# The second norm of a hybrid decoder layer, done by two parts of the tokens

## The chip, the cores and the metric

The kernel runs on one core of one Trainium2 chip. The metric is the device time of one execution in microseconds (us); lower is better. The kernel before takes 1798.79 us, the median of three runs (1796.71 to 1799.12).

The engines are named as in the profile: PE is TensorE's matmul, PEld its weight load, DVE VectorE, ACT ScalarE, POOL GpSimd, and SP the engine that issues most of the loads. L129 is line 129 of the kernel's file.

## The reference

One layer takes 256 prompt tokens and 8 x 8 sample tokens, 320 in all, of width 2048:

```python
h = rms_norm(x, p["norm_mix_pre"])
proj = h @ p["w_in"]
...
mix = jnp.concatenate([gate_out, ssm_out], axis=-1) @ p["w_out"]
x = x + rms_norm(mix, p["norm_mix_post"])
f, new_ffn_conv = conv_ffn(rms_norm(x, p["norm_ffn_pre"]), ffn_conv_state,
                           p["ffn_w_up"], p["ffn_conv_w"], p["ffn_conv_b"], p["ffn_w_down"])
x = x + rms_norm(f, p["norm_ffn_post"])
```

`gate_out` is a spatial gate over chunks of 128 tokens, `ssm_out` a scan over the tokens in four groups of heads with a state that is given back. `w_out` is 4096 x 2048; `conv_ffn` multiplies by `w_up` (2048 x 11264), runs a short convolution over the tokens, gates one half with the other and multiplies by `w_down`. All is float32. The change concerns the line that begins `x = x + rms_norm(mix`, which this text calls the second norm: each token's root mean square is over all 2048 channels of `mix`, so it can't be formed before the last of them is there.

## The kernel before

Tokens lie along the free axis. Each product has 128 x 128 weights as the stationary operand and 320 columns, one a token, as the moving one; channels lie across the 128 partitions, 16 blocks of them (`KD`).

To keep float32's accuracy each weight and each activation is split in a high and a low part of type fp32r, and `accumulate` (L127) makes three matmuls of one: high by high, high by low, low by high (L129, L130, L131). Each loads its weights.

`slab` (L110) brings in 512 KB of weights: a load that SP issues (L115), a copy on ACT that gives the high part (L118), a subtraction on DVE that gives the low part (L120). Three buffers each hold the raw, the high and the low slab.

The projection by `w_out` runs in eight chunks of its 4096 rows, as `chunk_out` (L205): for each of 16 blocks of output channels, 4 x 3 matmuls gather in one of four banks of PSUM (`mm`), and DVE adds the bank to the sum `acc` (L217). A slab serves two blocks. In the last chunk, number 7, a step of `squares_of` (L284) goes along with each block: ACT squares it (L281, and L300 for the last three), POOL or DVE adds the squares up (L282, L302).

Behind the last block comes the second norm: `token_sums` (L258) adds the squares over partitions, as f32 matmuls of one column against ones (three windows of 128 tokens, from 0, 128 and 192); `rsqrt_by_root` (L243) gives the root on DVE and ACT in seven short steps; `spread` (L267) turns each window's 128 roots into rows of 128 columns by three transposes into PSUM. From there `x1_ready` (L1035) takes one channel block after the other: normalise (DVE, L1040), add x (DVE for the first two blocks, POOL for the others, L1041), split for the FFN (ACT L346, DVE L347).

The FFN's first product runs through `project` (L153), with six banks filling at once (four of `mm`, two of `ms`): slabs of two channel blocks by 512 outputs, and slabs of four blocks by 256 outputs of the other half.

The order on each engine comes from a scheduler that goes by the order of the text, by priorities (`first()`, `tc.high_priority`) and by `tc.issue_after`, which puts an instruction behind another. Every engine works through its own list in that order. So that TensorE has something to do around the second norm, two pieces of the scan's last group are put there by hand: `end(3)` (two state products, two DVE additions, two stores of 256 KB on POOL's queue) and `final()` (a 512-column f32 product, L936, one addition and one store on POOL's queue).

The tile `hT` (a high and a low part of 16 blocks by 320 columns) holds the input of the big products. In chunk 7 its last four blocks hold that chunk's operand, and the first twelve have been read for the last time.

Of the kernel before, what the change touches and what calls it, by code (L numbers as in the profile page):

```python
# [17 lines left out]
P = 128  # L18
# [16 lines left out]
def hybrid_step(  # L35
# [72 lines left out]
    slab_load = []  # L108

    def slab(src, begins=False):  # L110
        n = src.shape[2]
        with tc.high_priority(offset=100000):
            m = n * src.shape[1]
            raw = wp.tile([P, 1024], F32, tag="wraw", name="wraw", bufs=3)
            slab_load.append(sp.dma_start(raw[:, :m].rearrange("p (a n) -> p a n", n=n), src).ins)  # L115
            hi = wp.tile([P, 1024], F32R, tag="whi", name="whi", bufs=3)
            for o in (slice(0, P), slice(P, m)) if begins else (slice(0, m),):
                act.copy(hi[:, o], raw[:, o])  # L118
            lo = wp.tile([P, 1024], F32R, tag="wlo", name="wlo", bufs=3)
            dve.tensor_tensor(out=lo[:, :m], in0=raw[:, :m], in1=hi[:, :m].bitcast(F32), op=ALU.subtract)  # L120
# [84 lines left out]
    def chunk_out(w, ck, hi, lo, begins, done=None, rate=1):  # L205

        for nb in range(KD):
            if nb % 2 == 0:
                wb = slab(rows_of(w, 4 * ck, 4, P * nb, 256))
            ps = mm.tile([P, 512], F32, tag="mm", name=f"pd_{ck}_{nb}")  # L210
            for k in range(4):
                made = accumulate(ps[:, :NT], wb(k, nb % 2), hi[:, k, :], lo[:, k, :], k == 0, k == 3)
            with first():
                if begins:
                    act.copy(acc[:, nb, :], ps[:, :NT])
                else:
                    dve.tensor_tensor(out=acc[:, nb, :], in0=acc[:, nb, :], in1=ps[:, :NT], op=ALU.add)  # L217
# [23 lines left out]
    rsqrt_ins, sums_ins = [], []  # L241

    def rsqrt_by_root(rest, ps, scale, rows=P):  # L243

        v = tp.tile([P, 3], F32, tag="rs_v3", name="rs_v")[:rows]
        r = tp.tile([P, 3], F32, tag="rs_r3", name="rs_r", bufs=3)[:rows]
        t = tp.tile([P, 3], F32, tag="rs_t3", name="rs_t")[:rows]
        s = tp.tile([P, 3], F32, tag="rs_s3", name="rs_s")[:rows]
# [9 lines left out]
    def token_sums(*sqs):  # L258

        ps = misc("tsum")  # L260
        for c, o in enumerate((0, P, NT - P)):
# [3 lines left out]
        return ps[:, 0:3]  # L265

    def spread(r, out=None):  # L267

        ps = misc("spread")
        for c, o in ((2, NT - P), (0, 0), (1, P)):  # L270
            pe.transpose(ps[:, o:o + P], r[:, c:c + 1].to_broadcast([P, P]), ident)
# [4 lines left out]
    def add_square(total, x, begins, adder=pool, place=("sq", 2)):  # L276
        if begins:
            act.activation(total, x, AF.Square)
        else:
            sq = tp.tile([P, NT], F32, tag=place[0], name="sq", bufs=place[1])  # L280
# [3 lines left out]
    def squares_of(total):  # L284
# [3 lines left out]
        def step(nb):  # L288
            if nb < KD - 3:
                add_square(total, acc[:, nb, :], nb == 0)  # L290
# [4 lines left out]
            with first():  # L295
                if nb < KD - 1:
                    held.append(misc("sq_ps")[:, :NT])
                else:
                    one.append(tp.tile([P, NT], F32, tag="sq", name="sq", bufs=2))
                act.activation((one or held)[-1], acc[:, nb, :], AF.Square)  # L300
                if nb > KD - 3:
                    dve.tensor_tensor(out=total, in0=total, in1=held.pop(0), op=ALU.add)  # L302
        return step, one

# [35 lines left out]
    def split(hi, lo, x, scale=None):  # L340

        if scale is None:
            act.copy(hi, x)
            dve.tensor_tensor(out=lo, in0=x, in1=hi.bitcast(F32), op=ALU.subtract)
        else:
            act.activation(hi, x, AF.Copy, scale=scale)  # L346
            dve.scalar_tensor_tensor(out=lo, in0=x, scalar=scale, in1=hi.bitcast(F32), op0=ALU.mult, op1=ALU.subtract)  # L347
# [16 lines left out]
    with ExitStack() as mctx:  # L364
# [341 lines left out]
        with tc.tile_pool(name="sd", bufs=1) as sd:  # L706
# [24 lines left out]
            rest = []  # L731

            def ssd(g):
# [138 lines left out]
                if g < 3:  # L872
                    end(3)
                    yield
# [59 lines left out]
                def final():  # L934
                    ps = misc("fin_ps")
                    made = pe.matmul(ps, btok[:, 1, bs], x1d, start=True, stop=True)  # L936
                    yield made.ins
# [3 lines left out]
                if g == 3:  # L941
                    rest.extend([lambda: end(3, pool), final()])
                else:
                    yield
                    yield
                    for _ in final():
                        pass
# [57 lines left out]
            chunk_out(w_out, 7, *res[3], False, squares)  # L1005
# [4 lines left out]

            with first():
# [12 lines left out]
                with tc.issue_after(made):  # L1024
                    r2b = spread(r)
# [254 lines left out]
```

## Time and profile before

| | |
|---|---|
| median of 3 runs | 1798.79 us (1796.71 to 1799.12) |
| the profiled execution's own time | 1800.87 us |
| its span, first to last instruction | 1799.2 us |
| granted TensorE clock, mean | 0.995 |
| PE, PEld busy | 1776.3 us (99%), 1741.7 us (97%) |
| DVE, ACT, POOL busy | 1190.1 (66%), 795.4 (44%), 295.4 us (16%) |
| read from HBM | 275.71 MB, 161 GB/s with what is written |

The span is one execution's; its own time has 1.67 us around it. Busy time of PE and PEld counts overlapping records, so a busy PE says little of its speed. The chain of waits lists, in order of time, what each step waited for: start, duration, engine, tile and line. A window's row gives the window, its length, then the busy us (and instructions) of PE, PEld, DVE, ACT and POOL, then PEclk, the granted TensorE clock as a share of full speed, the share of the DMA engines and GB/s. The timeline's rows are start, duration, engine, line, operation, output<-inputs, the stationary and moving shapes and the count; a bracket tells the idle time before and what ended it.

### The profile page before, as it was taken

How to read it: one execution, taken by the hardware profiler on the slowest of the kernel's cores; microseconds unless marked ns; L12 is line 12 of the kernel's file. 1: busy time of each engine (PE TensorE's matmuls, PEld its weight loads, DVE VectorE, ACT ScalarE, POOL GpSimd, SP SyncE). 2: the span in 40 equal slices, each digit the busy share in tenths (PEclk: the TensorE clock that was granted, in tenths of full speed). 3: DMA queues.
4: the chain of work that ended last, by engine and by line, in shares of the span. 5: the costliest groups of instructions: out<-in, count | busy, mean ns of one | idle time of the engine just before them, and what ended most of it. 6: DMA issues, size and time to landing. Idle time of an engine off the chain costs nothing.

```text
span 1799.2 us, 31167 instructions
## 1 busy us (share of the span) xinstructions
PE 1776.3 (99%) x12200; PEld 1741.7 (97%) x12200; DVE 1190.1 (66%) x2048; ACT 795.4 (44%) x1105; POOL 295.4 (16%) x619
## 2 busy tenths in 40 slices
PE   9999999999999999999999999999999999999998
PEld 8999999999889899999999999999999999999997
DVE  5458664556987969776875474747566565656575
ACT  6444454334545446445554433333434343433335
POOL 3102200000431313104331010111101020101004
PEclk9999999999999999999999999999999999999999
DMA  8646544455566574654554555455545554454542
GB/s 276 194 141 195 159 143 152 153 153 177 180 193 192 167 234 147 178 169 146 174 149 151 155 152 151 148 154 153 153 145 154 152 156 145 153 152 153 151 150 102
DMA packets 222226, 292.56 MB, mean 163 GB/s; under 512 B 16672, under 2 KB 150656, under 8 KB 221888
## 3 DMA queue, kind: packets, MB, share of 16 engines
q1 hardware_dynamic: 209392, 268.12, 49.3%
q10 hardware_dynamic: 10304, 14.82, 2.3%
q0 software_dynamic: 2384, 7.64, 1.4%
q8 instruction: 96, 1.57, 0.4%
q14 instruction: 50, 0.41, 0.1%
HBM read 275.71 MB, written 14.82 MB: 161 GB/s over the span
## 4 chain that ended last, share of the span: by engine, by line
PE 92%; DVE 4%; DMA 2%; issue 1%; ACT 1%; POOL 0%; ACTq 0%; DVEq 0%; POOLq 0%
PE ps L129 20%; PE ps L131 19%; PE ps L130 19%; PE pd L129 10%; PE pd L131 10%; PE pd L130 10%; DMA wraw<-in_w_in 1%; DVE wlo L120 1%; PE y_ps L910 1%; PE yo_ps L817 0%; PE up_ps L833 0%; PE sg L670 0%; ACT whi L118 0%; PE tsum L263 0%; PE vt_ps L582 0%
## 5 line engine op out<-in xcount | busy, mean ns | idle before, releaser
L120 DVE TENSOR_TENSOR wlo<-wraw,whi 128x1024 fp32r<-128x1024 f32 (+1 forms) x474 | 587.6, 1240 | 440.0 <-ACT whi L118 438.2
L118 ACT CAST whi<-wraw 128x1024 fp32r<-128x1024 f32 (+1 forms) x475 | 494.7, 1042 | 717.1 <-PE ps L130 414.8
L129 PE MATMUL ps<-h_hi,whi 128*128 128x320 f32 x2524 | 783.5, 311 | 4.0 <-ACT h_hi L346 2.1
L131 PE MATMUL ps<-h_hi,wlo 128*128 128x320 f32 x2524 | 781.4, 310 | 2.1 <-DVE wlo L120 1.9
L130 PE MATMUL ps<-h_lo,whi 128*128 128x320 f32 x2524 | 780.8, 309 | 0.0
L129 PEld LDWEIGHTS ps<-h_hi,whi 128*128 128x128 f32 x2524 | 475.6, 189 | 7.9 <-issue 2.7
L131 PEld LDWEIGHTS ps<-h_hi,wlo 128*128 128x128 f32 x2524 | 475.4, 188 | 4.1 <-DVE wlo L120 3.5
L130 PEld LDWEIGHTS ps<-h_lo,whi 128*128 128x128 f32 x2524 | 475.6, 188 | 0.7 <-DVE h_lo L546 0.2
L129 PE MATMUL pd<-fhi,whi 128*128 128x320 f32 x704 | 217.2, 309 | 0.0
L131 PE MATMUL pd<-fhi,wlo 128*128 128x320 f32 x704 | 217.2, 309 | 0.0
L130 PE MATMUL pd<-flo,whi 128*128 128x320 f32 x704 | 217.2, 308 | 0.0
L129 PE MATMUL pd<-ohi,whi 128*128 128x320 f32 x448 | 139.6, 312 | 0.0
L131 PE MATMUL pd<-ohi,wlo 128*128 128x320 f32 x448 | 138.4, 309 | 0.0
L130 PE MATMUL pd<-olo,whi 128*128 128x320 f32 x448 | 138.3, 309 | 0.0
L130 PEld LDWEIGHTS pd<-flo,whi 128*128 128x128 f32 x704 | 132.2, 188 | 0.0
L129 PEld LDWEIGHTS pd<-fhi,whi 128*128 128x128 f32 x704 | 132.2, 188 | 0.0
L131 PEld LDWEIGHTS pd<-fhi,wlo 128*128 128x128 f32 x704 | 132.2, 188 | 0.0
L1091 POOL COPY ptf<-pad 128x2 f32<-128x2 f32 x88 | 21.0, 238 | 621.1 <-DVE pad L1079 620.4
L217 DVE TENSOR_TENSOR acc_ffn<-acc_ffn,pd 128x320 f32<-128x320 f32 x160 | 77.6, 485 | 37.9 <-PE pd L131 36.4
L129 PEld LDWEIGHTS pd<-ohi,whi 128*128 128x128 f32 x448 | 84.1, 188 | 1.4 <-issue 0.6
L131 PEld LDWEIGHTS pd<-ohi,wlo 128*128 128x128 f32 x448 | 84.1, 188 | 0.5 <-issue 0.4
L130 PEld LDWEIGHTS pd<-olo,whi 128*128 128x128 f32 x448 | 84.2, 188 | 0.2
(301 smaller groups left out, 1592.3 us busy)
## 6 DMA issues: line engine op xcount, KB each, us to landing
wraw<-in_ffn_w_up SPq DMA_DIRECT2D x176, 512.0 KB, 3.7
wraw<-in_w_in SPq DMA_DIRECT2D x144, 512.0 KB, 3.7
wraw<-in_ffn_w_down SPq DMA_DIRECT2D x88, 512.0 KB, 3.5
wraw<-in_w_out SPq DMA_DIRECT2D x64, 512.0 KB, 3.5
st<-in_state_ssm SPq DMA_DIRECT2D x32, 256.0 KB, 4.5
out_ssm_state_sample<-st ACTq DMA_DIRECT2D x30, 256.0 KB, 4.6
cs<-dacs_d SPq DMA_DIRECT2D x16, 320.0 KB, 4.3
xr<-in_xT SPq DMA_DIRECT2D x4, 640.0 KB, 4.0
```

The lines of the kernel that those rows point to most:

```text
L118: act.copy(hi[:, o], raw[:, o])
L120: dve.tensor_tensor(out=lo[:, :m], in0=raw[:, :m], in1=hi[:, :m].bitcast(F32), op=ALU.subtract)
L129: pe.matmul(ps, whi, xhi, start=first, stop=False)
L130: pe.matmul(ps, whi, xlo, start=False, stop=False)
L131: return pe.matmul(ps, wlo, xhi, start=False, stop=last).ins
L217: dve.tensor_tensor(out=acc[:, nb, :], in0=acc[:, nb, :], in1=ps[:, :NT], op=ALU.add)
L910: pe.matmul(ps[64 * i:64 * i + 64, cols], w(hl), x(hl, m, cpx), tile_position=(0, 64 * i), **flags)
L1091: pool.tensor_copy(ptf[:, k, :], pad[:, 256:258])
```

## The change

The tokens are taken in two parts around the second norm, tokens 128 to 319 (192 columns) and tokens 0 to 127 (128 columns).

- Chunk 7 of the projection runs blocks 0 to 7 as before. Blocks 8 to 15 run once for the first part and then, with the same weights, once more for the second. Their four slabs stay in place for both: three in the free columns of `hT`, one in an ordinary buffer. Squares and sums go by part too.
- The first part's token sums stand behind two blocks of the second part, its spread behind five. The second part's token sums stand behind four products-of-three of the FFN, its spread behind ten.
- The FFN's first two slabs (two channel blocks by 512 outputs, four by 256) run for the first part and then for the second; `x1_ready` does channel blocks 0 to 3 by part. From there on it is 320 columns again, with the normalisation of the next two blocks put behind the split of a slab.
- `end(3)` and `final()` of the last group return to the scan's own order, as for the other groups, and their stores to ACT's queue.

```diff
+    def block_out(wb, nb, hi, lo, ts, begins, made=None):
+
+        ps = mm.tile([P, 512], F32, tag="mm", name=f"pd_{nb}")
+        for k in range(4):
+            ins = accumulate(ps[:, ts], wb(k, nb % 2), hi[:, k, ts], lo[:, k, ts], k == 0, k == 3)
...
+    PARTS = (slice(P, NT), FROM[1:]), (slice(0, P), FROM[:1])
+
+    def chunk_out_in_parts(w, ck, hi, lo, cut, kept, done, root, at):
+
+
+        pairs, step = {}, root(0)
+        for i, (ts, _) in enumerate(PARTS):
+            made = None
+            for nb in range(cut, KD):
+                if i and nb - cut in at:
+                    with tc.issue_after(last):
+                        made = next(step)
+                if not i and nb % 2 == 0:
+                    pairs[nb] = pair_of(w, ck, nb, kept.pop(0) if kept else None)
+                with tc.issue_after(made) if made else nullcontext():
+                    last = block_out(pairs[nb - nb % 2], nb, hi, lo, ts, False)
+                done(nb, ts, KD - 1 - nb)
+        return last
+
+    def root_in_parts(total, one, out):
+
+        def root(i):
+            of = PARTS[i][1]
+            with first():
+                most = token_sums(total, of=of)
+                ps = token_sums(one[i], of=of)
+                r = rsqrt_by_root(most, ps, 1.0 / D)
+                yield sums_ins[-1]
+                spread(r, of=of, ps=out)
+                yield spread_ins[-1]
+        return root
...
-                if g < 3:
-                    end(3)
-                    yield
+                end(3)
+                yield
...
-                    (pool if g == 3 else act).dma_start(o_ssm_p[g], s1)
+                    act.dma_start(o_ssm_p[g], s1)
...
-            chunk_out(w_out, 7, *res[3], False, squares)
+            kept = [[h.rearrange("p k n -> p (k n)")[:, 12 * NT - 1024 * i:][:, :1024] for h in hT] for i in (3, 2, 1)]
+            r2p = misc("spread")
+            root = root_in_parts(sq2, one, r2p)
+            chunk_out(w_out, 7, *res[3], False, squares, blocks=range(8))
+            last = chunk_out_in_parts(w_out, 7, *res[3], 8, kept, squares, root, (2, 5))
...
-            with first():
-                with tc.issue_after(pd_last[-1]):
-                    made = rest[0]()
-                with tc.issue_after(made):
-                    most = token_sums(sq2)
-                with tc.issue_after(sums_ins[-1]):
-                    ps = token_sums(*one)
-                with tc.issue_after(sums_ins[-1]):
-                    made = next(rest[1])
-                r = rsqrt_by_root(most, ps, 1.0 / D)
-                behind = rsqrt_ins[-1]
-                with tc.issue_after(behind):
-                    next(rest[1])
-                with tc.issue_after(made):
-                    r2b = spread(r)
...
-            project(ffn_w_up, 0, None, late=up0, ready=x1_ready, after=behind, ahead=1, more=DFF, held=added)
...
+            x1_ready(0, 4, PARTS[0][0])
+            s0 = up_slab(0, 2, 0, 4)
+            m0 = up_slab(0, 4, 4, 2)
+            step = root(1)
+            for ts, _ in PARTS:
+                n = 0
+                for wb, ks, js in (s0, (0, 1), four), (m0, (0, 1, 2, 3), two):
+                    made = last
+                    products = up_products(wb, 0, ks, js, ts)
+                    while True:
+                        with tc.issue_after(made):
+                            last = next(products, None)
+                        if last is None:
+                            last = made
+                            break
+                        made, n = last, n + 1
+                        if ts == PARTS[0][0] and n in (4, 10):
+                            with tc.issue_after(made):
+                                last = made = next(step)
+                            if n == 10:
+                                x1_ready(0, 4, PARTS[1][0])
...
+            for k0 in range(2, KD - 4, 2):
+                all_of(behind_slab(k0 + 2, 2 if k0 + 2 < KD - 4 else 4, k0, 2, 0, 4), k0, (k0, k0 + 1), four)
+                if k0 % 4 == 2 and k0 > 2:
+                    all_of(up_slab(k0 - 2, 4, 4, 2), k0 - 2, range(k0 - 2, k0 + 2), two)
```

More of the change, by code (lines that the diff above doesn't have):

```diff
@@ L264, in token_sums, with spread @@
         sums_ins.append(ins)
[L265 to L271, printed above, removed]
+        return ps[:, 0:len(of)]
+    def spread(r, out=None, of=FROM, ps=None):
+        if ps is None:
+            ps = misc("spread")
+        for c in sorted(range(len(of)), key=lambda c: -(of[c] % P)):
+            spread_ins.append(pe.transpose(ps[:, of[c]:of[c] + P], r[:, c:c + 1].to_broadcast([P, P]), ident).ins)
         if out is not None:
@@ L935, in final @@
                     ps = misc("fin_ps")
[L936 to L937 removed]
+                    pe.matmul(ps, btok[:, 1, bs], x1d, start=True, stop=True)
+                    yield
                     dve.tensor_tensor(out=s1, in0=s1, in1=ps, op=ALU.add)
[L939 removed]
+                    act.dma_start(o_ssm_p[g], s1)
                     yield
[L941 to L947, printed above, removed]
+                yield
+                yield
+                for _ in final():
+                    pass
             tasks = [ssd(g) for g in range(4)]
@@ new lines, in hybrid_step @@
+            four, two = list(enumerate(range(4))), list(enumerate((4, 5)))
+            x1_ready(0, 4, PARTS[0][0])
[19 more added lines that the diff above has]
+                                x1_ready(0, 4, PARTS[1][0])
@@ L1050, in hybrid_step @@
+            k0 = KD - 4
+            for j0 in (0, 2, 4):
+                all_of(up_slab(k0, 4, j0, 2), k0, range(k0, KD), list(enumerate((j0, j0 + 1))))
+            with tc.issue_after(x1_split[7][0]), tc.issue_after(x1_split[-1][1]):
                 for kt in range(KD):
```

116 lines of the change are left out of this document (68 added, 48 removed).

## The prediction

> **What bounds the kernel now.** I read the page first, then the chain of waits around the second norm, then single windows with their granted clock, then the timeline of TensorE's matmuls (PE) and weight loads (PEld).
>
> ```profile
> span 1799.2 us, 31167 instructions
> PE 1776.3 (99%) x12200; PEld 1741.7 (97%) x12200; DVE 1190.1 (66%) x2048; ACT 795.4 (44%) x1105; POOL 295.4 (16%) x619
> ```
>
> TensorE is the bound. The busy share hides what a matmul costs: the rows give 0.31 us each, but they overlap, and in the timeline one 320-column product starts 0.147 us after the other (835.82, 835.96, 836.11, ...). The page's 12200 matmuls have 12200 weight loads: each product loads its weights anew. The second norm is a hole in this stream:
>
> ```profile
> 843.13 0.47 ACT sq L300
> ...
> 843.65 0.84 PE tsum L263 x6
> ...
> 845.76 0.56 PE spread L271 x3
> ...
> 846.35 1.01 DVE acc_mix L1040 x2
> 847.35 0.41 DVE acc_mix L1041
> ...
> 847.78 0.57 ACT h_hi L346
> ...
> 848.40 0.64 PE ps L129
> ```
>
> The chain runs from the last square over the token sums, the root (seven short steps between 844.51 and 845.72), the spread and the first split to the first product of the FFN at 848.40. The last product of the projection started at 841.98. The windows show a second cost, the clock (column PEclk, after the five engines' busy us):
>
> ```profile
> 842.12:848.40 6.28, 3.52 (x22) 2.27 (x20) 5.43 (x16) 2.24 (x5) 1.67 (x3) 0.90 0.58 206
> 848.40:854.00 5.60, 5.60 (x21) 5.60 (x22) 5.16 (x9) 4.03 (x10) 4.14 (x4) 0.51 0.20 36
> ...
> 34.74:38.16 3.42, 2.38 (x15) 1.85 (x13) 1.06 (x1) 2.14 (x4) 0.00 (x0) 1.00 1.09 336
> 38.16:41.57 3.41, 3.19 (x22) 3.19 (x23) 0.30 (x2) 3.34 (x6) 0.49 (x3) 1.00 0.81 238
> 239.54:242.96 3.42, 3.02 (x26) 2.52 (x25) 2.58 (x8) 1.40 (x2) 0.00 (x0) 1.00 0.52 155
> 242.96:246.37 3.41, 3.41 (x14) 3.41 (x14) 0.30 (x2) 0.54 (x3) 0.47 (x2) 0.50 0.40 142
> 843.70:847.12 3.42, 2.28 (x11) 1.21 (x11) 2.57 (x10) 0.20 (x1) 1.65 (x3) 1.00 0.50 185
> 847.12:850.53 3.41, 2.13 (x8) 2.13 (x9) 3.41 (x7) 2.42 (x6) 1.13 (x2) 0.50 0.20 77
> ```
>
> After the hole the clock is at 0.5 until 853.94, and a product takes 0.267 us. It halves in steps of 3.41 us, after a step with little work. Work is not busy time: 239.54:242.96 has TensorE busy 88% (tiny matmuls of 32 to 128 columns), and the clock halved; 34.74:38.16 has it busy 70% with 320-column products, and the clock stayed. Streamed columns sort them. At half clock 320 columns take 0.267 us, 1.2 per ns, so full speed is 2.4 per ns (320 in 0.133, and 0.014 from product to product) and 8190 in a step. 34.74:38.16 has 13 products of 320, 51%; 843.70:847.12 has four passes of 512 for the f32 product (an f32 matmul leaves two records, each of two passes) and the spread, 30 to 34%; 239.54:242.96 some 30%. So the bound lies between 34 and 51%. That this is what the clock follows is my inference from these windows.
>
> The price of a short matmul:
>
> ```profile
> 843.64 0.74 PEld L263 LDWEIGHTS tsum<-ones,sq 128*128 128x128 f32 x6 [0.43 <-ACT sq L300]
> ...
> 657.30 0.19 PEld L130 LDWEIGHTS ps<-h_lo,whi 128*128 128x128 f32 x1
> 657.41 0.19 PEld L131 LDWEIGHTS ps<-h_hi,wlo 128*128 128x128 f32 x1
> ...
> 242.91 0.28 PEld L129 LDWEIGHTS ps<-h_hi,whi 128*128 128x128 f32 x1
> 243.07 0.34 PEld L130 LDWEIGHTS ps<-h_lo,whi 128*128 128x128 f32 x1
> ```
>
> Six token sums of one column load weights every (0.74 - 0.19) / 5 = 0.11 us; two loads of the split weights (fp32r) at 657 stand 0.11 apart as well. A matmul of one column therefore costs as much as a load, 0.11 us. With the clock at half the loads stand 0.16 apart (242.91, 243.07).
>
> **The change, step by step.** The sum starts at the profiled execution: span 1799.2, its own time 1800.87, which is 2.1 above the median of the runs, 1798.79. I add the difference to the median.
>
> The hole goes: -5.65. Of 842.12 to 848.40 (6.28 us) useful work takes 3.14: the group's two state products 0.46, twelve token-sum records 1.33, the last state product of 512 columns in f32 1.02, the spread 0.33. Lost: 3.14. From 848.40 to 854.00, 21 products take 5.60 instead of 21 x 0.147 = 3.09. Lost: 2.51. The two state products and the last one (1.48 us of PE) move up beside the scan of the last group; there they cost the same, and they filled the hole before, so 1.48 stays paid. With them go two state additions and one addition on DVE (0.68 each, DVE 66% busy) and three 256 KB stores, from POOL's queue to ACT's (ACT 44% busy; nothing reads them back): 0.
>
> 144 products become two: +10.9. Eight blocks x 4 x 3 = 96, and 48 of the first slabs, run as 192 and as 128 columns. By columns they would take 0.093 and 0.066 us (2.4 per ns and 0.013 from one to the next); the weight load of 0.11 is longer than both. Each pair costs 2 x 0.1115 instead of 0.147, 0.076 more. No row has such products in fp32r. Bounds: by columns alone 0.013 more a pair, 1.9 us in all; as f32, where a record of 320 columns takes 0.27 and one of 128 0.112, two each, 0.41 more a pair, 59 us. I take the load's step, since the fp32r loads at 657 show it.
>
> [...]
>
> Two groups of sums and of spreads instead of one: +0.3, two more changes between short f32 and long products at some 0.1 to 0.15 (656.85 to 657.56).
>
> Waits that stay: +0.8 (0 to 3). The chain of part one has three blocks of part two (4.0 us) after its sums and three before its first use; from the rows (normalising step 0.54 at 320 columns, so 0.41 at 192, addition 0.3, split 0.56 and 0.5) DVE works until some 5.6 us after the first spread, while the last three blocks and three products end at 5.3. DVE does things in order, so the evacuations of the last blocks queue behind this chain, and the fourth FFN bank waits for the last of them: some 0.6. The root of part two (1.25 us) has six products-of-three (2.0 us) and the split six more: 0.2. Seven slabs come one per block (1.76 us) instead of one per two, each 3.5 us from issue to landing with three buffers; DVE may wait for them, and four PSUM banks (5.3 us) cover that: 0, up to 2 if they don't. The 16 smaller evacuations, squares and splits are ACT, DVE and POOL work beside PE; SP loads the same slabs.
>
> Without the clock: -5.65 + 10.9 + 0.3 + 0.8 = +6.4, 1805.2.
>
> The clock falls: +6.5 (0 to 14). 128 columns per 0.1115 us are 1.15 per ns, 48%; 192 are 72%. Part one's token sums (eight records, 0.9 us of nearly no columns) lie among the 128-column blocks. A step of 3.41 us that holds them has (3.41 - 0.9) x 0.48 / 3.41 = 35%, about what halved the clock at 843.70; one that holds half of them some 42%. At half clock a product of 128 or 192 columns costs 0.17, 0.058 more, and streams only 32% or 47%, so the clock may not come back before the 320-column products. After the sums come 72 products of 128 (at most +4.2), then 48 of 192 and 48 of 128 (up to +5.6), and two steps of 320 at 0.267 (+1.5 each). Running these numbers over the place where the steps fall and a bound between 34 and 51%, most cases lie between +5 and +8.5, the longest at +14. I take +6.5.
>
> Sum: +12.9, 1811.7. Only +6.4 of it is from rows without inference.
>
> **The rivals.**
> The first: the clock holds (bound below 35%, or steps that fall well): 1805.2, from 1803 to 1808. For it: 34.74:38.16 stayed at 1.00 with 51%. Against: 843.70 and 239.54. [...]
>
> The second, not slower: loads of short fp32r products hide behind the columns. Then the pairs cost 1.9 and PE streams over 80%, the clock holds: -5.65 + 1.9 + 0.3 + 0.8 = -2.7, 1796.1. It decides where such products follow each other in under 0.089 us (288 x 0.089 = 144 x 0.147 + 5.65 - 1.1). Against: in the token sums and state products no load of 128 weights follows another in under 0.107. Even with the hole gone and pairs free it can't pass -5.65.
>
> The third: short fp32r products run like f32, +59 in place of +10.9, 1853 with the rest. Against: the loads at 657 are as short as others and every product leaves one record.
>
> **How the numbers follow.** Clock falls 0.60, holds 0.20, not slower 0.15, as f32 or a stall of another kind 0.05. Prediction 1811.7. The range 1801 to 1821 takes in both first cases with their waits and leaves out 0.2. A measurement of this kernel tells some 0.2% (3.6 us) from no change: the second rival lies within or just beyond that, so its 0.15 goes to faster with 0.07 and to the same with 0.08, and slower has 0.85.
>
> **What would show it.** Products of 128 and 192 columns 0.11 us apart at full clock (0.066 and 0.093 if wrong); no chain of 6 us between projection and FFN; the clock 0.5 in some step from the second block of tokens 0 to 127 on, ending in the 320-column products; waits for the evacuation of the last blocks under 1 us. Wrong it would be by a step under 0.089, a clock that holds at 35%, or a PE wait over 3 us for slabs.

## The result, and the profile after

The changed kernel takes 1814.35 us (median of 7 runs, 1805.02 to 1821.94) against 1798.79 for the kernel before (7 runs, 1796.71 to 1805.07). The ratio is 1.0079, with a 95% interval from 1.0058 to 1.0100. It is slower by some 14 to 16 us; 1811.7 was forecast, with a range from 1801 to 1821. The runs of the changed kernel spread much wider than those before, and the slower ones tend to the lower mean TensorE clock (0.989 at 1821.94, 0.998 at 1805.02).

The page of the profiled execution (1816.31 us, span 1814.6):

```profile
span 1814.6 us, 31505 instructions
PE 1794.1 (99%) x12344; PEld 1761.4 (97%) x12344; DVE 1192.6 (66%) x2074; ACT 794.5 (44%) x1116; POOL 293.8 (16%) x623
...
PEclk9999999999999999997999999999999999999999
```

TensorE has 144 matmuls more and 17.8 us more busy time, the other engines nearly the same as before (VectorE 1192.6 us for 1190.1). The row of granted clock has one digit below 9, in the slice that holds the second norm. The hole between projection and FFN is gone: in the timeline of TensorE, products of 128 columns, with the first part's sums and spread between them, follow each other up to the first FFN product at 856.48, which comes 0.21 us after the last one of the projection. Instead there is this (start, duration, then engine, line and operands; L131 to L133 of the changed kernel are L129 to L131 of the kernel before):

```profile
842.83 0.27 PE L133 MATMUL pd<-h_hi,h_lo 128*128 128x128 f32 x1
842.94 0.27 PE L131 MATMUL pd<-h_hi 128*128 128x128 f32 x1
843.05 0.28 PE L132 MATMUL pd<-h_lo,h_hi 128*128 128x128 f32 x1
843.16 0.38 PE L133 MATMUL pd<-h_hi,h_lo 128*128 128x128 f32 x1
843.33 0.42 PE L131 MATMUL pd<-h_hi 128*128 128x128 f32 x1
843.55 0.42 PE L132 MATMUL pd<-h_lo,h_hi 128*128 128x128 f32 x1
843.77 0.41 PE L133 MATMUL pd<-h_hi,h_lo 128*128 128x128 f32 x1
```

The starts are what counts: 0.11 us apart until 843.16, 0.17 across the change of clock at 843.19, and 0.22 behind it. The windows, cut where the clock changes (columns as before: the five engines' busy us with instructions, the granted clock, the DMA share, GB/s), show why:

```profile
839.77:843.18 3.41, 3.41 (x33) 3.41 (x32) 1.47 (x8) 0.82 (x3) 0.91 (x2) 1.00 0.00 0
843.18:846.60 3.42, 3.42 (x19) 3.42 (x17) 0.65 (x3) 0.39 (x2) 0.46 (x1) 0.50 0.00 0
...
856.84:860.25 3.41, 3.41 (x18) 3.41 (x18) 0.49 (x3) 0.34 (x2) 0.00 (x0) 0.50 0.00 0
860.25:863.66 3.41, 3.41 (x18) 3.41 (x17) 0.64 (x4) 0.17 (x1) 0.00 (x0) 0.50 0.00 0
863.66:867.00 3.34, 3.34 (x32) 3.34 (x32) 2.58 (x9) 2.10 (x5) 1.10 (x2) 1.00 0.01 2
```

TensorE is busy 100% of every one of them, and yet the clock is at half from 843.19 to 863.67, six steps of 3.41 us.

Where the time went can be counted. I take the stretch from the first product of block 8 of the last projection chunk to the first product behind the first FFN group, and add the distances from each TensorE start to the next by kind of product (us; full-clock distances are 0.1467 for 320 columns, in both profiled executions, and 0.1117 for a short product):

| part of the stretch | before | after | difference |
|---|---|---|---|
| 320-column products at full clock | 384, 56.33 | 240, 35.21 | -21.12 |
| short products at full clock | 0 | 288, 32.17 | +32.17 |
| what half clock adds to products | 2.59 | 9.30 | +6.71 |
| sums, root, spread, state products, waits for them | 6.46 | 2.01 | -4.45 |
| waits among the 320-column products | 0 | 1.56 | +1.56 |
| sum | 65.39 | 80.25 | +14.87 |

The state products that left this stretch are found ahead of it: from the first state product of the last scan group (`s_ps`) to block 8 it is 117.86 us before and 119.00 after, +1.14. The last TensorE product comes 14.55 us later than before and not 16.0, since the profiled execution of the changed kernel happened to reach the last scan group 1.49 us sooner; the end behind it is 0.9 us longer.

The 1.56 us of waits is a row that the kernel before does not have, a split of weights that VectorE finishes late:

```profile
881.94 0.31 PE L132 MATMUL ps_up<-h_lo,whi 128*128 128x320 f32 x1
882.65 0.42 PE L133 MATMUL ps_up<-h_hi,wlo 128*128 128x320 f32 x1 [0.40 <-DVE wlo L121]
```

### The profile page after: what moved, and what is told of

Its sections match the earlier page's. It is cut to its first block, busy times and chain, and to the rows that moved or that the text cites. A ratio compares the mean times of both kernels' runs of the same rounds, so it can differ in the third digit from the quotient of the medians.

```text
span 1814.6 us, 31505 instructions
## 1 busy us (share of the span) xinstructions
PE 1794.1 (99%) x12344; PEld 1761.4 (97%) x12344; DVE 1192.6 (66%) x2074; ACT 794.5 (44%) x1116; POOL 293.8 (16%) x623
## 4 chain that ended last, share of the span: by engine, by line
PE 90%; DVE 5%; DMA 3%; ACT 1%; issue 1%; POOL 0%; SPq 0%; DVEq 0%; ACTq 0%; POOLq 0%
PE ps L131 19%; PE ps L133 18%; PE ps L132 18%; PE pd L131 10%; PE pd L132 10%; PE pd L133 10%; DMA wraw<-in_w_in 2%; DVE wlo L121 2%; ACT whi L119 1%; PE y_ps L962 1%; DMA cs<-dacs_d 1%; PE up_ps L886 0%; PE yo_ps L870 0%; PE sg L724 0%; PE tsum L279 0%
## 5 line engine op out<-in xcount | busy, mean ns | idle before, releaser
L131 PE MATMUL ps<-h_hi,whi 128*128 128x320 f32 x2428 | 753.2, 310 | 2.7 <-DVE acc_mix L224 1.0
L133 PE MATMUL ps<-h_hi,wlo 128*128 128x320 f32 x2428 | 750.7, 309 | 1.0 <-DVE wlo L121 0.9
L132 PE MATMUL ps<-h_lo,whi 128*128 128x320 f32 x2428 | 750.3, 309 | 0.0
L131 PEld LDWEIGHTS ps<-h_hi,whi 128*128 128x128 f32 x2428 | 456.1, 188 | 6.1 <-issue 2.5
L133 PEld LDWEIGHTS ps<-h_hi,wlo 128*128 128x128 f32 x2428 | 455.9, 188 | 2.4 <-DVE wlo L121 1.7
L132 PEld LDWEIGHTS ps<-h_lo,whi 128*128 128x128 f32 x2428 | 456.1, 188 | 1.0 <-issue 0.2
L133 PE MATMUL pd<-fhi,wlo 128*128 128x320 f32 x704 | 217.2, 309 | 0.0
L131 PE MATMUL pd<-fhi,whi 128*128 128x320 f32 x704 | 217.2, 309 | 0.0
L131 PE MATMUL pd<-ohi,whi 128*128 128x320 f32 x448 | 140.8, 314 | 0.0
L133 PE MATMUL pd<-ohi,wlo 128*128 128x320 f32 x448 | 139.4, 311 | 0.0
L131 PEld LDWEIGHTS pd<-fhi,whi 128*128 128x128 f32 x704 | 132.2, 188 | 0.0
L133 PEld LDWEIGHTS pd<-fhi,wlo 128*128 128x128 f32 x704 | 132.2, 188 | 0.0
L131 PEld LDWEIGHTS pd<-ohi,whi 128*128 128x128 f32 x448 | 84.7, 189 | 1.4 <-issue 0.6
L133 PEld LDWEIGHTS pd<-ohi,wlo 128*128 128x128 f32 x448 | 84.8, 189 | 0.1
```

Source lines behind the costliest of these rows:

```text
L131: pe.matmul(ps, whi, xhi, start=first, stop=False)
L132: pe.matmul(ps, whi, xlo, start=False, stop=False)
L133: return pe.matmul(ps, wlo, xhi, start=False, stop=last).ins
```

## Experiments

Three questions: is the price of the short products as the prediction has it; does the clock follow the columns streamed in a step; and is the hole worth what was put down for it.

### The short products alone

```
-                made = accumulate(ps[:, :NT], wb(k, nb % 2), hi[:, k, :], lo[:, k, :], k == 0, k == 3)
+            for ts in (slice(P, NT), slice(0, P)) if <blocks 8 to 15 of chunk 7> else (slice(0, NT),):
+                for k in range(4):
+                    made = accumulate(ps[:, ts], wb(k, nb % 2), hi[:, k, ts], lo[:, k, ts], k == 0, k == 3)
```

> The kernel before, with nothing changed but the matmuls of blocks 8 to 15 of chunk 7: each product of 320 columns becomes one of 192 and one of 128 into the same bank (96 products become 192). The norm, its hole, the moved work and the slabs stay as before. If a short product costs a weight load (0.111 us in the profile of after), each pair costs 0.222 instead of 0.147: +7.3 us, 1806, and the products of 192 and of 128 stand 0.111 apart; the two sizes alternate every 1.3 us, so 60% of full speed is streamed and the clock holds there. If the time of after came from waits or from the moved work instead and short products cost their columns, +1.3 us (800 to 1801 in the last three digits and the thousands: 1800 to 1801).

Measured: 1804.69 us (1803.08 to 1807.74) against 1798.26, ratio 1.0045, interval 1.0030 to 1.0060: +6.4 us by the medians, +8.1 by the ratio, and the interval, 5.4 to 10.8 us, holds the expected 7.3. The timeline:

```profile
839.75 0.28 PE L129 MATMUL pd<-h_hi,whi 128*128 128x128 f32 x1
839.87 0.28 PE L130 MATMUL pd<-h_lo,whi 128*128 128x128 f32 x1
839.98 0.27 PE L131 MATMUL pd<-h_hi,wlo 128*128 128x128 f32 x1
```

In its stretch 96 products of 192 and 96 of 128 columns take 10.91 and 10.47 us, 0.114 and 0.109 each. Around the norm the clock halves only behind the hole, at 850.78 for 6.83 us, as in the kernel before. So the price of a pair is shown by itself: a product of 128 columns costs as much as one of 192, and as much as the 0.11 us from one weight load to the next.

### The norm's chain taken out

```
-                with tc.issue_after(made):
-                    most = token_sums(sq2)
-                with tc.issue_after(sums_ins[-1]):
-                    ps = token_sums(*one)
...
-                r = rsqrt_by_root(most, ps, 1.0 / D)
-                behind = rsqrt_ins[-1]
+                behind = pd_last[-1]
...
-                    r2b = spread(r)
+                r2b = r1
```

> The kernel before without the second norm's token sums, root and spread; the normalisation takes the rows of the first norm instead (left out: the second norm's root, so the values behind it differ). It measures what the hole can give at most. The chain that made PE wait is gone, the two state products and the last one stay where they were. If the hole costs what the prediction worked out, idle time and half clock go (-5.65), and the sums and the spread themselves (-1.66): 1791.5, clock 1.00 around the end of chunk 7. If the hole hides something that takes its place (the splits of the first slabs or blocks, which are ready no earlier), less: 1794 to 1797.

Measured: 1800.28 us (1797.13 to 1801.67), ratio 1.0009, interval 0.9999 to 1.0019. No gain: a miss for my step. The hole was still there, with another cause:

```profile
839.77 0.62 PE L833 MATMUL up_ps<-xsp,bm 128*128 128x512 f32 x2
845.94 2.07 PE L936 MATMUL fin_ps<-xde,btok 128*128 128x512 f32 x2 [5.54 <-DVE sq L302]
847.02 1.25 PE L129 MATMUL ps<-h_hi,whi 128*128 128x320 f32 x1
```

Free to start early, the normalisation of the finished blocks filled VectorE ahead of time, and the square additions (L302) that free the PSUM bank of the last state product came 5.54 us late. The clock halved too, at 843.98 for 6.83 us. The run replaces one wait by another and says nothing on the worth of the hole; a later run does.

### Columns and the clock, in the second part and in the sums

Two kernels, each the changed one with more columns in one place. In the first, the second part of the projection streams 192 columns, 64 of them unread:

```
+            wide = slice(0, 192) if ts.stop == P else ts
-            ins = accumulate(ps[:, ts], ..., hi[:, k, ts], lo[:, k, ts], k == 0, k == 3)
+            ins = accumulate(ps[:, wide], ..., hi[:, k, wide], lo[:, k, wide], k == 0, k == 3)
```

> The kernel after, with the second part's 96 matmuls in the projection streaming 192 columns (tokens 0 to 191) instead of 128; the 64 more are not read. The same instructions in the same order, more columns in each. If the clock follows streamed columns (the steps of 3.41 us that halved it in the profile of after had some 36%), those steps now have over 50% and the clock holds: products stay 0.111 apart because the load is longer than both sizes, the 10 us of half clock go, 1805, and the runs lie close together. If the clock falls because matmuls are short or many, or because of the token sums alone, it falls as before: 1812 to 1816. If short products cost by their columns, +2.6 us on after (0.027 x 96).

Measured: 1809.14 us (1808.05 to 1811.12), ratio 1.0066, interval 1.0049 to 1.0083. The clock stayed at 1.00 through the whole stretch, as the theory of columns has it, but the time is 4 us above its number. At full clock a wait shows that half clock had hidden, for the PSUM banks that the last blocks leave late:

```profile
852.79 0.28 PE L133 MATMUL ps_up<-h_hi,wlo 128*128 128x192 f32 x1
854.04 0.36 PE L131 MATMUL ps_up<-h_hi,whi 128*128 128x192 f32 x1 [0.98 <-DVE acc_mix L225]
...
854.88 0.36 PE L131 MATMUL ps_up<-h_hi,whi 128*128 128x192 f32 x1 [0.25 <-DVE acc_mix L225]
```

These waits are only a small part of the 4 us. Beside the run that comes next, whose clock held as well, the profiled execution is 5.3 us longer: 1.0 of it lies in the stretch of the table (72.73 us for 71.70) and 4.2 ahead of the last scan group, where the two kernels are the same. What made that part longer stays open.

In the second, only the token sums of the second norm stream 128 columns of ones instead of one:

```
-                ins = pe.matmul(ps[:, c:c + 1], sq[:, o:o + P], ones[:, 0:1], ...)
+                ins = pe.matmul(ps[:, P * c:P * c + P], sq[:, o:o + P], ones, ...)
```

> The kernel after, with the second norm's token sums streaming 128 columns of ones instead of one (the same sums in every column; six matmuls of f32, which load as long as before). If the token sums' 0.9 us of nearly no columns are what takes a step of 3.41 us below the bound, the steps now have 48% or more and the clock holds: 1805. If 48%, the share of 128-column products alone, is too little already, the clock falls as in after: 1812 to 1816, starting at the end of the first step that has only 128-column products.

Measured: 1805.19 us (1803.27 to 1806.36), ratio 1.0045, interval 1.0030 to 1.0060. The expected number to 0.2 us, and the clock at 1.00 where it had been at 0.50:

```profile
836.00:840.00 4.00, 4.00 (x39) 4.00 (x37) 1.44 (x5) 1.02 (x4) 0.46 (x1) 1.00 0.00 0
840.00:845.00 5.00, 5.00 (x48) 5.00 (x47) 2.17 (x10) 1.13 (x4) 1.37 (x3) 1.00 0.00 0
...
836.81:840.22 3.41, 3.41 (x34) 3.41 (x32) 0.93 (x4) 0.98 (x3) 0.61 (x2) 1.00 0.00 0
```

The products and their order are those of the changed kernel; only the eight small records of the first sums and the four of the second carry more columns, at the same 0.11 us each. The last row is a step that matches the one that halved the clock before: in 836.81 to 840.22, as in 839.77 to 843.18 of the changed kernel, 23 products of 128 columns and the eight records of the sums start, and TensorE is busy throughout. That the sums tip the clock is shown by this pair. It also gives the change without the clock's fall: its stretch takes 71.70 us, 6.3 more than before, with 2.9 us of waits in it (1.3 for the banks, 1.6 for weight splits).

### Both parts 160 columns wide

```
-    PARTS = (slice(P, NT), FROM[1:]), (slice(0, P), FROM[:1])
+    PARTS = (slice(160, NT), (160, NT - P)), (slice(0, 160), (0, 32))
```

> The changed kernel with its two parts cut at token 160 instead of 128: every short product streams 160 columns, none 192 or 128. The number of products is the same; the second part has two windows of token sums instead of one, four small records more (+0.4 us). Theory (the clock follows the columns streamed in a step of 3.41 us, bound between 35 and 37.5%): 160 columns per 0.111 us are 60% of full speed, a step that holds 0.9 us of token sums as well has (3.41 - 0.9) x 0.60 / 3.41 = 44%, so the clock holds through the region, a product still costs its weight load of 0.111, and the time is that of the changed kernel without the fall, 1805 to 1806.5. Rival (the clock falls whenever products are paced by their weight loads, or when token sums interrupt them): it falls again, 1812 to 1816. Second rival (160 columns cost more than a load, or the pair isn't paced by the loads): another step than 0.111 between products.

Measured: 1821.11 us (1820.34 to 1821.69), ratio 1.0121, interval 1.0101 to 1.0141. A miss, and the slowest of all. The product's price held (starts 0.11 apart, so the second rival is out). The clock fell, but not where the rival put it:

```profile
844.28:847.70 3.42, 3.42 (x33) 3.42 (x32) 1.61 (x8) 0.88 (x3) 0.89 (x3) 1.00 0.00 0
847.70:851.11 3.41, 3.41 (x33) 3.41 (x33) 2.05 (x7) 1.11 (x3) 1.52 (x3) 1.00 0.00 0
...
854.52:857.94 3.42, 2.70 (x20) 2.39 (x21) 1.43 (x6) 0.91 (x3) 0.00 (x0) 1.00 0.02 5
857.94:861.35 3.41, 3.41 (x18) 3.41 (x18) 0.65 (x4) 0.20 (x1) 0.00 (x0) 0.50 0.00 0
```

The step 844.28 to 847.70 holds the first sums and 23 products of 160 columns, 45% of full speed (an estimate: 2.4 columns per ns, twice the 320 in 0.267 us of half clock), and the clock held, as computed. The step that tipped it is 854.52 to 857.94: there the waits for late banks and the second group of sums, twice as long as in the changed kernel, fall together, and only some 12 products run, 23%:

```profile
855.43 0.34 PE L131 MATMUL ps_up<-h_hi,whi 128*128 128x160 f32 x1 [0.36 <-DVE acc_mix L224]
...
856.35 0.34 PE L131 MATMUL ps_up<-h_hi,whi 128*128 128x160 f32 x1 [0.36 <-DVE acc_mix L224]
...
856.75 0.98 PE L279 MATMUL tsum<-ones,sq 128*128 128x1 f32 x8
```

At half clock 16 products of 160 columns, 31%, then go through each step, and it took until the 320-column products for the clock to come back, 20.48 us later. The expectation forgot the waits that full clock brings, though the run above had just shown them. In the traces the stretch is 15.9 us longer than before, the scan ahead of it 1.5, what lies before that 1.3 and the end behind the last product 0.9, together about the 19.5 us between the two profiled executions; the medians stand 23 apart mostly because the profiled execution of the kernel before (1800.87) lies 2.7 above the median that this run is compared with.

### The state products back in the scan

```
-                if g < 3:
-                    end(3)
-                    yield
+                end(3)
+                yield
...
-                if g == 3:
-                    rest.extend([lambda: end(3, pool), final()])
-                else:
...
-                    made = rest[0]()
```

> The kernel before, with only one part of the change done: the last group's two state products, its last product, their additions and stores go back into the scan's own order, out of the hole. My step: they cost TensorE 1.48 us there as they did in the hole, where they were free, and the hole doesn't get shorter, since its chain runs from the last square over sums, root and spread: +1.5, 1800.1. Rival: the scan has idle TensorE time that takes them, 1798.6. Second rival: the hole gets shorter because the token sums no longer stand behind them, 1798 to 1799.

Measured: 1799.11 us (1796.15 to 1805.64) against 1798.14, ratio 1.0006, interval 0.9992 to 1.0020. The median is 1.0 above; the interval tells it neither from 1.5 nor from nothing. The trace does: the scan up to block 8 takes 119.10 us instead of 117.86, +1.24, and the hole is as long as it was:

```profile
841.37 0.80 PE L263 MATMUL tsum<-ones,sq 128*128 128x1 f32 x6 [0.22 <-DVE sq L302]
842.50 0.83 PE L263 MATMUL tsum<-ones,sq 128*128 128x1 f32 x6 [0.33 <-ACT sq L300]
844.62 0.54 PE L271 MATMUL spread<-ident,rs_r 128*128 128x128 f32 x3 [1.29 <-DVE rs_r L255]
847.26 0.90 PE L129 MATMUL ps<-h_hi,whi 128*128 128x320 f32 x2 [2.09 <-ACT h_hi L346]
```

From the last product of the projection (840.84) to the first of the FFN it is 6.42 us, and 6.42 in the kernel before (841.98 to 848.40). The wait for the root grew by what the last product of the state had filled (0.3 to 1.29).

### The hole filled

```
             ps += [misc(f"ps_{c0}_{j}") for j in range(nb, nb + 2)]
+            with first():
+                made = spread_last[-1]
+                for _ in range(8):
+                    with tc.issue_after(made):
+                        made = pe.matmul(ps[0][:, 384:512], ones, ones, start=True, stop=True).ins
```

> The kernel before, with eight more f32 products of 128 columns (ones by ones, into unread columns of the first FFN bank) right behind the second norm's spread, 8 x 0.22 = 1.8 us of TensorE in the 2.0 us in which it waits for the first split. Nothing else changes. Theory (streamed columns): they add 4096 columns to the step of 3.41 us that had 30 to 34%, so the clock no longer halves behind the hole, and the 2.51 us of products at half clock go: 1796.0 to 1796.5 against 1798.6. Rival one (the clock follows the idle time or the waits, which stay): no gain, 1798.6. Rival two (the fill runs over the 2.0 us and pushes the first product of the FFN back): 1799 to 1800.

Measured: 1799.34 us (1797.03 to 1806.55), ratio 1.0001, interval 0.9989 to 1.0014: no gain, and by neither of the rivals. The fill fits, and the clock holds behind it (timeline of TensorE):

```profile
851.84 1.95 PE L163 MATMUL ps<-ones 128*128 128x128 f32 x16
854.10 1.15 PE L129 MATMUL ps<-h_hi,whi 128*128 128x320 f32 x6 [0.30 <-ACT h_hi L351]
...
879.48 0.31 PE L130 MATMUL ps<-h_lo,whi 128*128 128x320 f32 x1
881.02 0.42 PE L131 MATMUL ps<-h_hi,wlo 128*128 128x320 f32 x1 [1.23 <-DVE wlo L120]
```

The 2.59 us of half clock are gone, and 2.76 us of waits have come among the 320-column products, the longest at 879.48, where the kernel before waits for nothing. The stretch takes 65.37 us, before 65.39. The windows (third busy column: VectorE) say who is behind:

```profile
860.00:865.00 5.00, 5.00 (x36) 5.00 (x36) 5.00 (x7) 1.82 (x4) 2.69 (x2) 1.00 0.48 168
...
875.00:880.00 5.00, 4.79 (x33) 4.53 (x31) 5.00 (x7) 2.72 (x5) 4.05 (x6) 1.00 0.33 105
```

Behind the hole VectorE normalises 16 blocks, splits them and splits the weights, and is busy 4.4 to 5.0 us of every 5; in the kernel before it is busy as much (4.45 to 5.00 of each 5 us from 854 to 884), but there TensorE comes late enough to find the splits done. By these rows the hole has a second limit right behind it. Whether that is VectorE alone, the last four kernels below ask.

### The hole taken out, with VectorE kept free

```
 (the kernel without the norm's chain, and:)
+                evac_last.append(dve.tensor_tensor(out=acc[:, nb, :], ...).ins)
...
-                    with first() if kt < 2 else tc.high_priority(offset=100000):
+                    with first() if kt < 2 else tc.high_priority(offset=100000), tc.issue_after(evac_last[-5 if kt < 2 else -1]):
```

> The kernel before without the second norm's sums, root and spread (the first norm's roots stand in for the second's, so that part is left out of the computation), as in the run without the root, but with the normalisation of the first two blocks held behind the evacuation of the projection's block 11 and that of the others behind the last block, so that VectorE isn't filled ahead of time. My step: the hole is worth 3.14 us of idle TensorE and 2.51 us at half clock, so without it 1798.6 - 5.65 = 1793; with the waits of the first split behind the last evacuations at most 1 to 2 us more, 1793 to 1795. Rival (the hole is worth less, since something else is late right behind it): 1797 to 1799, and the trace shows which wait it is.

Measured: 1796.09 us (1794.55 to 1804.23), ratio 0.9992, interval 0.9978 to 1.0006. The stretch takes 63.96 us, 1.4 less than before; 5.65 was my step. The clock held and nothing of the norm's chain stands between the products; the waits of TensorE in the stretch, by who was waited for (us in total, times, longest), are:

```profile
PE ps L131 <- DVE wlo L120: 3.3, 2, 1.8
PE fin_ps L936 <- DVE sq L302: 0.6, 1, 0.6
PE ps L130 <- DVE h_lo L347: 0.2, 1, 0.2
```

The list gives the time between records, 4.1 us; by the distances from start to start, as in the table, the waits are 6.1. The run leaves out the sums and the spread as well (1.66 us), so that some 7.3 us were to be won, and 1.4 were. With this and the filled hole it is shown that taking the hole away wins little of its cost here: four fifths came back as waits, all of them for results of VectorE.

### Less work on VectorE

Four kernels with the normalising product left out for blocks 6 to 15: the kernel before, the filled hole, the early normalisation, and the changed kernel with wide sums.

```
+                        if kt < 6:
-                        dve.scalar_tensor_tensor(out=a, in0=a, ..., in1=r2b, op0=ALU.mult, op1=ALU.mult)
+                            dve.scalar_tensor_tensor(out=a, in0=a, ..., in1=r2b, op0=ALU.mult, op1=ALU.mult)
```

> The kernel before, with the second norm's product (block times weight times root) left out for blocks 6 to 15 of the 16, so that VectorE has ten instructions of 0.5 to 1.0 us less between the hole and the end of the first FFN group; nothing of that group's TensorE work is touched. It is the control for the next two. New theory (behind the hole stands a second limit: VectorE, busy 45 of 49 us from the spread on, whose weight splits are nearly late already): in the kernel before TensorE hardly waits there (0.2 us), so there is nothing to win: 1798.0 against 1798.2. Rival (VectorE's load costs time in the kernel before as well): 1795 to 1797.

> The kernel with the filled hole, with the same ten VectorE products left out. With the hole filled the clock held, but TensorE waited 2.4 us more for the weight splits behind it, and the end of the first FFN group came as late as before. New theory (the gain at the hole was given back to VectorE's backlog): with less work on VectorE the 2.5 us appear, 1795.7 against 1798.0 of the control. Rival (loads of the slabs, or ScalarE, pace the group): no gain, 1798.

> The kernel without the second norm's root and with the early normalisation, with the same ten VectorE products left out. There TensorE waited 6.1 us in all where the hole had been and behind it, 2.5 of it for weight splits from 867 us on. New theory: those 2.5 us go, the waits right behind the last block (3.6 us: a bank, the first splits, the split at 848.59 behind four products that are still there) stay: 1793.6 against 1796.1 with them and 1798.0 of the control. Rival (something other than VectorE paces the group): 1796.

> The changed kernel with token sums of 128 columns (its clock held), with the same ten VectorE products left out. There TensorE waited 1.0 us for evacuations at the start of the FFN and 1.6 us for weight splits behind it. New theory: the 1.6 us go and the 1.0 stays: 1803.6 against 1805.2, which is what the short products cost beside what the hole was worth. Rival (these waits come from the loads): 1805.2.

Measured, against 1800.78 of the kernel before on that chip: 1803.15 (ratio 1.0008, 0.9992 to 1.0024), 1800.65 (0.9985, 0.9970 to 1.0000), 1799.70 (0.9987, 0.9971 to 1.0003) and 1812.53 (1.0056, 1.0039 to 1.0073). The stretches take 66.52, 66.52, 64.04 and 74.73 us: none is shorter than with the work left in (65.39, 65.37, 63.96 and 71.70), and the one of wide sums is 3.0 longer. So the numbers expected of less VectorE work did not come: four misses. The control itself, expected at 1798.0, came at 1803.15; beside it the second and the third are 2.5 and 3.5 us lower, near what was expected of the difference, but the second one's stretch is as long as the control's, so its gain does not lie there. In the traces the order of the other engines has changed with it. The waits of TensorE and of ScalarE and the timeline of GpSimd, with the hole filled:

```profile
PE ps L129 <- ACT whi L118: 0.8, 1, 0.8
```

```profile
ACT h_hi L351 <- POOL acc_mix L1047: 8.4, 7, 3.4
```

```profile
854.85 10.28 POOL L1047 TENSOR_TENSOR acc_mix<-acc_mix,xr 128x320 f32<-128x320 f32 x8 [2.00 <-DMA xr<-in_xT]
```

GpSimd's additions, 1.28 us each, now stand in one queue, behind a wait of 2.00 us for the load of x; ScalarE's splits of blocks (`h_hi`) wait for them, and the splits of weight slabs (`whi`) wait behind those in ScalarE's order. In the kernel with wide sums that is one wait of 2.0 us, and the clock halves for one step behind it (881.33, 3.41 us), which adds 1.1. VectorE is where the waits end in the kernels that have all their work; that it alone sets the pace is not shown, since taking its work away moved the wait to ScalarE and GpSimd. The rivals on record, ScalarE and the loads, are not ruled out.

## Why the prediction was right, point by point

**What bounds the kernel: right.** TensorE, 99% before and after; of the 15.4 us between the two profiled spans 14.55 are in its own starts.

**The hole goes, -5.65: the size is right at its place, and its worth was not seen.** In the table the hole, its half clock and the short chain that replaces them come to 6.46 + 2.59 - 2.01 = -7.04, where the steps (-5.65, -1.48 for the products that move, +0.3 for the second group of sums) had -6.83. But the step took this as won. The filled hole and the early normalisation show that a second limit stood right behind: of such a gain, most comes back. In the changed kernel less of it does, 1.56 us. Four blocks are normalised in parts ahead of time there, and VectorE has the long half-clock stretch to catch up; that these are the reasons is not tested.

**The moved products, still paid: right.** 1.48 forecast; 1.14 in the changed kernel's trace and 1.24 in the run that moves nothing else.

**144 products become two, +10.9: right.** +11.05 in the table (32.17 - 21.12). The second rival (loads hidden by columns, 0.089 us or less a product) is out: no stream of 128, 160 or 192 columns ran faster than 0.109 on average. So is the third, f32-like products.

**Waits that stay, +0.8: too small by half, and at other places.** 1.56 us in the changed kernel, all for weight splits of VectorE, which the prediction had put at 0 with up to 2; the waits for the last blocks' banks, which it named, are 0 there, where TensorE runs at half clock. At full clock they are 1.3 us (wide sums), and 1.8 in the run with two parts of 160.

**The clock falls, +6.5: the reading by streamed columns fits, the size was too small.** It measures +9.30, and some 0.4 more in the sums and spreads. Two terms were mis-sized. A short product at half clock was put at 0.17 us, from one pair of weight loads 0.16 apart; in the stream it is 0.213, for 128, 160 and 192 columns alike, nearly twice the 0.111 of full clock. And the fall was to last to the 320-column products or to be over soon; it lasted six steps and ended among the 192-column products, after a step with 16 of them. The bound, set between 34 and 51%, can now be set closer, as an estimate. By counted starts, at 2.4 columns per ns for full speed, a step with 23 products of 128 columns and eight sums (36% of full speed, 839.77 to 843.19) halved the clock, and steps with 39, 40, 45 and 47% did not (10 products of 192 and 10 of 128 with wide sums; 17 of 192 with four sums and two bank waits in the run with the wide second part; 23 of 160 with seven sums; 30 of 128). Back to full it went after a step with 37.5% (16 of 192 at half clock), and not after 27, 28 or 31%. One bound of 36 to 37.5% fits all of these. They are steps of products with 128 x 128 weights; for the scan's products with narrower weights (64 columns and fewer) the count is not settled. The step before 598.27 in the run with the wide second part, 3.42 us with TensorE busy 1.83, comes to some 30% if each record's columns are counted once and to 50% if twice, and the clock halved. That an f32 record counts twice, as the prediction has it, fits the wide products of the kernel before: f32 records of 320 columns (`x1p`) start 0.270 us apart, the split ones 0.147; f32 records of 512 (`fin_ps`, `s_ps`; two a product) 0.43 to 0.53, those of `up_ps` 0.22.

**The first rival, the clock holds: 1805.2 was right as a number.** The wide sums make it true, 1805.19, though of the terms in it waits of 2.9 stand for the 0.8 + 0.3 forecast, and chance has a part in the agreement to 0.01. The two fastest runs of the changed kernel, 1805.02 and 1808.91 at a mean clock of 0.998, are near where this rival has them. No trace was taken of them, but a mean of 0.998 leaves some 5 to 9 us at half clock in the whole execution (an estimate: twice the 0.15 to 0.25% that are missing of some 1805 us), and in the traces the end of the execution alone has 4 to 8 us of it. So the fall around the norm was short in these two, or was not there: what the clock costs differs from one execution of the changed kernel to the next.

The sum, +12.9, came out at +16.0 in the traces (14.87 + 1.14) and +15.6 by the medians. The forecast of 1811.7 is 2.6 below, by the clock's term almost alone. One reading in the prediction is wrong without bearing on the sum: between 844.51 and 845.72 stand six of the root's seven steps, the first is at 843.92.

## What to carry to other kernels

Splitting the 320-column products into 192 and 128 columns bought overlap here at the price of the weight load: 288 starts at 0.111 us for 144 at 0.147, 11 us to save a hole of 6. Before a hole is priced, read the busy share of the engines that feed the stretch behind it: where one of them is busy all the time, the hole may be time that the feeding needs, and what is won at the hole can come back as waits, here within some 30 us. And read the columns that each step streams beside the busy share: eight records of one column among products of 128 halved the clock here with TensorE busy 3.41 us of 3.41; the same records with 128 columns, at the same 0.11 us each, kept it at 1.00.

## What the runs showed of the hardware

- The clock halved after a step in which TensorE had no idle time in the records (839.77 to 843.18: busy 3.41 us of 3.41, the clock 0.50 behind it). Widening the sums' records from 1 to 128 columns, with no other change, kept it at 1.00.
- All halvings but the one that runs past the end of each execution last a multiple of one length, 3.41, 6.83 or 20.48 us, and start at other places from run to run (the first ones of four kernels at 242.96, 481.37, 598.27 and 478.41). Within an execution their starts lie whole multiples of 3.4133 us apart: 604.16 us, 177 steps, between the first two of the kernel before, and 361.81 us, 106 steps, in the changed kernel. That the place of the steps decides how long a stretch near the bound stays at half clock would explain the 17 us between the fastest and the slowest run of the changed kernel; this is an inference, since no trace of either was taken.
- In a stream of products that each load 128 x 128 weights, one of 128 to 192 columns starts on average 0.109 to 0.114 us after the other at full clock (three widths, five kernels) and 0.213 at half clock; one of 320 columns 0.147 and 0.267.
